# One order for the high and the low matmul of a weight tile, in every contraction step

## The chip, the cores and the metric

The kernel runs on one core of one Trainium2 chip. The metric is the device time of one execution in microseconds (us). A shorter stretch is given in nanoseconds (ns) where that reads better.

## What is computed

One transformer-like block on 256 tokens of 2048 features, depth 1, in fp32: a gated feed-forward layer, a hybrid mixer (a gated short convolution beside a chunked state-space scan), a second feed-forward layer, a per-layer embedding gate and a last norm.

```python
def swiglu(x, w_in, w_out):
    g, u = jnp.split(x @ w_in, 2, axis=-1)
    return (jax.nn.silu(g) * u) @ w_out

def reference(x, p, ...):
    h = x
    for i in range(DEPTH):
        h = h + 0.5 * swiglu(rmsnorm(h, ffn1_norm[i]), ffn1_w_in[i], ffn1_w_out[i])
        h = h + hybrid_mixer(rmsnorm(h, mix_norm[i]), mix_w_in[i], ...)
        h = h + 0.5 * swiglu(rmsnorm(h, ffn2_norm[i]), ffn2_w_in[i], ffn2_w_out[i])
        gate = jax.nn.sigmoid(rmsnorm(h, ple_norm[i]) @ ple_w_gate[i])
        h = h + gate * (p[i] @ ple_w_proj[i])
    return rmsnorm(h, final_norm)
```

The weights are large (the feed-forward width is 5632) and every weight is used once.

## The kernel before

Activations lie with features on the partitions and the 256 tokens along the free axis. To keep fp32 accuracy with the faster float32r products, each operand is split into a high part and a low part. An activation tile of the right-hand side holds both, 256 columns of high next to 256 columns of low. A weight chunk of four contraction tiles (128 x 4 x 256) is loaded by SyncE (L95), copied to its high part on ScalarE (`hi`, L99), and the low part is the difference, made on VectorE (`lo`, L100). There are four raw buffers and three buffers of each part.

`Gemm` (L104 to L133) accumulates 256 output features, two halves of 128 called j = 0 and 1, each in a PSUM bank of its own. For each contraction tile k of a chunk it issues two matmuls: `hi` times both halves of x, 512 columns, over the whole bank; and `lo` times the high half of x, 256 columns, into the bank's second half. The tile numbers of a Gemm run chunk by chunk, in a chunk first all k of j = 0 and then all k of j = 1. At the last contraction tile of an accumulation the two matmuls are swapped, so that the wide one comes last and carries the stop mark:

```python
todo = [(acc, wh, x), (acc[:, T:], wl, x[:, 0:T])]
if k == self.K - 1:
    todo.reverse()
```

In TensorE's queue that gives hi, lo, hi, lo and so on, and once in each accumulation lo, lo, hi, hi: the last two tiles' low matmuls next to each other, then the last high one next to the first high one of what follows. There are 391 such accumulations. Those of the feed-forward and the mixer's input projection have 14, 15 or 16 contraction tiles, those of the mixer's output projection 32. The tail of the program (`one=True`) and the small projection `pr` use three narrow matmuls of 256 columns and have no swap.

`gather` (L138) drains an accumulator: ScalarE reads its second half (`elo`, L141), VectorE adds the first (`esum`, L143). Accumulators are double-buffered. A norm has `nps` (TensorE, L185), `nv` (VectorE, L202), `nrt` (GpSimd, L204), `npb` (TensorE, L208) and `r` (L211) in a row, with a few products of the next Gemm placed between `nps` and `npb`. The scan of the mixer puts small fp32 matmuls (`cb`, `xt`, `st`, `ab`, `yp`) between stretches of the projection's products; `st` reads `xe` (VectorE, L350).

The program is written with a scheduling framework. It lays out each engine's queue before the run, from priorities and from its own estimate of when operands will be ready; the weight splits have a raised priority (L98). So an edit in one place can move instructions of other engines.

Of the kernel before, what the change touches and what calls it, by code (L numbers as in the profile page):

```python
# [14 lines left out]
P = 128  # L15
T = 256
# [9 lines left out]
KC = 4  # L26
NEG = -1.0e30

# column tiles of mix_w_in in the order in which they are computed
C_B, C_C, C_X, C_Z, C_XS, C_BM, C_CM, C_DT = 0, 2048, 4096, 6144, 8192, 10240, 10752, 11264  # L30
MIX_ORDER = [("bc", i, C_BM + i * P) for i in range(8)]
MIX_ORDER += [("xs", i, C_XS + i * P) for i in range(16)]
# [5 lines left out]
Z_ORDER = [("z", i, C_Z + i * P) for i in range(16)]  # L38
ALL_ORDER = MIX_ORDER + SC_ORDER + Z_ORDER

# columns of the packed per-feature parameters
S_N1, S_NM, S_N2, S_NP, S_NF, S_SN, S_D = (16 * i for i in range(7))
S_SC = 112
S_CW = S_SC + 48
# [5 lines left out]
def block_kernel(ctx, tc, xT, pT, small, dtp, w1, o1, wm, wdt, om, w2, o2, wg, wp, out):  # L50
# [12 lines left out]
    def aux(name):  # L63
        return aux_p.tile([P, 512], F32, tag="aux", name=name)

    # ---- inputs and constants
    warm = cst.tile([P, 1], F32, name="warm")
    V.memset(warm, 0.0)
    A.activation(out=warm, in_=warm, func=AF.Exp)
# [19 lines left out]
    half = cst.tile([P, 2], F32, name="half")  # L89
    G.memset(half, -0.5)  # L90

    # ---- weights: load, split into two float32r parts
    def parts(src, nk, cols):
        w = raw.tile([P, KC, 256], F32, tag="w", name="w")
        nc.sync.dma_start(out=w[:, :nk, :cols], in_=src)  # L95
# [6 lines left out]
        return hi, lo  # L102

    class Gemm:  # L104
        """src [P, K, cols]; rhs(k) -> [P, 512] (high | low). One bank per 128 columns:
        [:256] the high products, [256:] the cross products (or all of them in [:256])."""

        def __init__(self, src, K, rhs, cols=256, one=False, acc=None):
            self.src, self.K, self.rhs, self.cols, self.one = src, K, rhs, cols, one
# [2 lines left out]
        def chunk(self, k0, k1):  # L112
            hi, lo = parts(self.src[:, k0:k1, :], k1 - k0, self.cols)
            for j in range(self.cols // P):
                js = slice(j * P, (j + 1) * P)
                for k in range(k0, k1):
                    x, acc = self.rhs(k), self.acc[:, j, :]
                    wh, wl = hi[:, k - k0, js], lo[:, k - k0, js]
                    if self.one:
                        todo = [(acc[:, 0:T], wh, x[:, 0:T]), (acc[:, 0:T], wh, x[:, T:]),  # L120
                                (acc[:, 0:T], wl, x[:, 0:T])]
                    else:
                        todo = [(acc, wh, x), (acc[:, T:], wl, x[:, 0:T])]
                        if k == self.K - 1:
                            todo.reverse()
                    for n, (o, a, b) in enumerate(todo):
                        nc.tensor.matmul(o, lhsT=a, rhs=b, start=(k == 0 and n == 0),  # L127
                                         stop=(k == self.K - 1 and n == len(todo) - 1))
# [7 lines left out]
        return Gemm(*args, **kw).all()  # L136

    def gather(acc, n=2, scale=1.0):  # L138
        """The sum of an accumulator's two halves, times scale, in SBUF."""
        lo = ev.tile([P, 2, T], F32, tag="elo", name="elo")  # L140
        A.mul(out=lo[:, :n, :], in_=acc[:, :n, T:], mul=scale)  # L141
        s = ev.tile([P, 2, T], F32, tag="esum", name="esum")
        V.scalar_tensor_tensor(out=s[:, :n, :], in0=acc[:, :n, 0:T], scalar=scale,  # L143
                               in1=lo[:, :n, :], op0=ALU.mult, op1=ALU.add)
        return s

    def split(dst, src, w=None):
        """dst [P, 512] f32r = high | low part of src (times the column w)."""
        if w is None:
            A.copy(out=dst[:, 0:T], in_=src)  # L150
            V.tensor_tensor(out=dst[:, T:], in0=src, in1=dst[:, 0:T].bitcast(F32), op=ALU.subtract)
        else:
            A.activation(out=dst[:, 0:T], in_=src, func=AF.Copy, scale=w)
            V.scalar_tensor_tensor(out=dst[:, T:], in0=src, scalar=w,  # L154
                                   in1=dst[:, 0:T].bitcast(F32), op0=ALU.mult, op1=ALU.subtract)
# [7 lines left out]
        return r.unsqueeze(1).to_broadcast([P, 2, T])  # L163

    class Norm:
        """Sums squares over features as they come; r = 1/sqrt(mean + eps) over partitions."""

        def __init__(self, n, tag):
            self.n, self.tag, self.acc, self.more = n, tag, None, None
# [15 lines left out]
                nc.tensor.matmul(ps[c], lhsT=src[:, c * P:(c + 1) * P], rhs=ones[:, 0:1], start=start, stop=stop)  # L185

        def begin(self):
            """All but the last tile's share, ahead of it."""
            self.ps = [aux("nps")[:, 0:1] for _ in range(NCH)]
            self.total(self.acc, self.ps, True, False)  # L190

# [20 lines left out]
            return (pbs[0], r) if both else r  # L212

    def next_x(src, m, x, wcol, norm):
        """Two finished tiles of h: their squares, and their parts for the next product."""
        norm.add(src)
        if x is not None:
            for i in range(2):
                split(x(m + i), src[:, i, :], sm[:, wcol + m + i:wcol + m + i + 1])

    # ---- feed-forward
    def ffn(wi, wo, x, norm, wcol_next, begun=()):
        xn, nn, r = None, Norm(D, "rn"), None
        f0 = 0
# [35 lines left out]
    for m in range(0, KD, 2):  # L260
        n1.add(h[:, m:m + 2, :])
    xm, nm = ffn(w1, o1, x1, n1, S_NM, first)
    # ---- mixer
    XT = blk.tile([P, KD, T], F32, tag="blk", name="XT")
    Xd = blk.tile([P, NCH, D], F32, tag="blk", name="Xd")
    ya = [blk.tile([P, 8, 512], F32R, tag="blk", name=f"ya{i}") for i in range(2)]
    BC = tmp.tile([P, 8, T], F32, name="BC")

    def conv(dst, src, wcol, taps, bias=None, func=None):
        """Causal over the free axis, one feature a partition."""  # L270
        c = ev.tile([P, T], F32, tag="t1", bufs=5, name="cv")
        w = lambda i: sm[:, wcol + i:wcol + i + 1]
        t = dst if func is None else c
        if bias is None:
            A.activation(out=t, in_=src, func=AF.Copy, scale=w(taps - 1))
        else:
            A.activation(out=t, in_=src, func=AF.Identity, scale=w(taps - 1), bias=bias)
        for d in range(1, taps):
            V.scalar_tensor_tensor(out=t[:, d:], in0=src[:, :T - d], scalar=w(taps - 1 - d),
                                   in1=t[:, d:], op0=ALU.mult, op1=ALU.add)  # L280
        if func is not None:
            A.activation(out=dst, in_=t, func=func)
# [17 lines left out]
            dst = XT[:, q, :] if kind == "xs" else BC[:, q, :]  # L300
            conv(dst, s[:, j, :], S_CW + 4 * ch, 4, bias=sm[:, S_CB + ch:S_CB + ch + 1], func=AF.Silu)

    # step sizes, in [head, token]
    s = gather(gemm(wdt, KD, xm, cols=P), n=1)
    dx = ev.tile([HEADS, T], F32, tag="t1", bufs=5, name="dx")
    V.tensor_tensor(out=dx, in0=s[:HEADS, 0, :], in1=rm[:HEADS, :], op=ALU.mult)
# [4 lines left out]
    an = tmp.tile([HEADS, 1], F32, name="an")  # L311
    A.activation(out=an, in_=dtv[:, 1:2], func=AF.Exp)
    V.tensor_scalar(out=an, in0=an, scalar1=-1.0, scalar2=None, op0=ALU.mult)
    # log(1 + e) = 2 atanh(e / (2 + e))
    sr = ev.tile([HEADS, T], F32, tag="t1", bufs=5, name="sr")
    V.tensor_scalar(out=sr, in0=e, scalar1=2.0, scalar2=None, op0=ALU.add)
    V.reciprocal(out=sr, in_=sr)
# [11 lines left out]
    V.tensor_scalar(out=dA, in0=dt, scalar1=an, scalar2=None, op0=ALU.mult)  # L329

    def ssd_group(g):
        # B C^T of the group, [s, l], and its B with tokens on partitions
        ps = aux("cb")
        for c in range(NCH):
            cs = slice(c * P, (c + 1) * P)
            nc.tensor.matmul(ps[:, cs], lhsT=BC[:, g, cs], rhs=BC[:, 4 + g, cs], start=True, stop=True)  # L336
        nc.tensor.transpose(ps[:, T:T + P], BC[:, g, 0:P], ident)
        CB = tmp.tile([P, 3, P], F32, tag="CB", bufs=2, name="CB")
        A.copy(out=CB.rearrange("p c l -> p (c l)"), in_=ps[:, 0:3 * P])
        for c in range(NCH):  # L340
            ps = aux("xt")
            for j in range(4):
                nc.tensor.transpose(ps[:, j * P:(j + 1) * P], XT[:, 4 * g + j, c * P:(c + 1) * P], ident)  # L343
            V.tensor_tensor(
                out=Xd[:, c, g * 512:(g + 1) * 512].rearrange("p (h d) -> p h d", d=HD),
                in0=ps.rearrange("p (h d) -> p h d", d=HD),
                in1=dtT[:, c, 0, g * 8:(g + 1) * 8].unsqueeze(2).to_broadcast([P, 8, HD]),
                op=ALU.mult)
        xe = ev.tile([P, 512], F32, tag="xe", bufs=1, name="xe")
        V.tensor_tensor(  # L350
            out=xe.rearrange("p (h d) -> p h d", d=HD),
            in0=Xd[:, 0, g * 512:(g + 1) * 512].rearrange("p (h d) -> p h d", d=HD),
            in1=dec[:, g * 8:(g + 1) * 8].unsqueeze(2).to_broadcast([P, 8, HD]),
            op=ALU.mult)
        ps = aux("st")
        nc.tensor.matmul(ps, lhsT=CB[:, 2, :], rhs=xe, start=True, stop=True)  # L356
        st = ev.tile([P, 512], F32, tag="st", bufs=1, name="st")
        A.copy(out=st, in_=ps)
        return CB, st
# [36 lines left out]
                in1=yp[:, a].rearrange("p c l -> p (c l)"), op0=ALU.mult, op1=ALU.add)  # L396

    def token_major():
        # token-major steps, and their running sums
        ps = aux("dtT")  # L400
        for c in range(NCH):
            for i, t in enumerate((dt, dA, dA)):
# [5 lines left out]
        for c in range(NCH):  # L408
            nc.tensor.matmul(ps[:, c * HEADS:(c + 1) * HEADS], lhsT=tri, rhs=dtT[:, c, 1, :], start=True, stop=True)
        for c in range(NCH):  # L410
            # running sums by head, twice over the partitions
            nc.tensor.matmul(ps[0:2 * HEADS, T + c * P:T + (c + 1) * P],
                             lhsT=dtT[:, c, 1:3, :].rearrange("p i h -> p (i h)"), rhs=tri,
                             start=True, stop=True)
# [8 lines left out]
        A.activation(out=dec, in_=ps[:, 2 * HEADS:3 * HEADS], func=AF.Exp)  # L423
        return dtT, acs, dec, sums

    # gated short convolution, the scan beside it
    for j in range(0, 16, 2):
        cvs = ev.tile([P, 2, T], F32, tag="cvs", bufs=1, name="cvs")
        for i in range(2):
# [16 lines left out]
            gst = ssd_group(g)  # L446
        ssd_heads(g, hh, *gst)

    # gate and group norm
    yb = []  # L450

    def group_norm(g, ng):
# [31 lines left out]
        V.tensor_tensor(out=hm, in0=s, in1=hm, op=ALU.add)  # L484
        next_x(hm, m, x2, S_N2, n2)

    # ---- second feed-forward
    xp, np_ = ffn(w2, o2, x2, n2, S_NP)

    # ---- per-layer embedding gate, final norm  # L490
    nf, rp = Norm(D, "rn"), None
    pin = ev.tile([P, 2, T], F32, tag="xe", bufs=1, name="pin")
    G.dma_start(out=pin, in_=pT)
# [47 lines left out]


def _layout(inp):
    """The inputs in the order in which the chip reads them: slices, transposes, repeats."""
    import numpy as np

    c = np.ascontiguousarray

    def tiled(w):
        """[K, N] -> [N/256, 128, K/128, 256]"""  # L550
        k, n = w.shape
        return c(w.reshape(k // P, P, n // 256, 256).transpose(2, 1, 0, 3))

    def gated(w):
        """Columns of gate and value side by side, 128 of each."""
        k = w.shape[0]
        return c(w.reshape(k // P, P, 2, KF, P).transpose(3, 1, 0, 2, 4)).reshape(KF, P, k // P, 256)

    def feat(v, per=1):
        """[per, F] -> [128, F/128 * per]"""  # L560
        v = np.asarray(v).reshape(per, -1, P)
        return v.transpose(2, 1, 0).reshape(P, -1)

# [39 lines left out]
```

## Time and profile before

| what | value |
|---|---|
| median of three timed runs | 2353.78 us (2353.03 to 2354.49) |
| the profiled execution, first to last instruction (span) | 2350.7 us |
| that execution's own device time | not listed; the median lies 3.1 us above the span |
| TensorE busy with matmuls | 2328.5 us, 99% of the span, 13,340 matmuls |
| TensorE loading weights | 2014.7 us, 86% |
| VectorE, ScalarE, GpSimd busy | 64%, 48%, 1% |
| granted TensorE clock, mean | 0.998 of full speed |
| mean busy share of the DMA queue that loads the weights (q1) | 60.6% |

The page's busy time of TensorE counts a matmul from its start to a modelled end, so matmuls overlap; what a matmul costs is read from the distance of its start to the next one's start.

### The profile page before, as it was taken

The numbers are of one execution on the slowest core, as the hardware profiler recorded it, in microseconds if no ns is written. First come the engines' busy times: TensorE is split into PE (matmuls) and PEld (weight loads), VectorE is DVE, ScalarE is ACT, GpSimd is POOL, SyncE is SP. The second block draws the span as 40 slices with busy tenths as digits, with TensorE's granted clock in tenths as the row PEclk, the third lists the DMA queues.
The fourth block names the chain that finished last, engine by engine and source line by source line (L and its number), as shares of the span: only waits on it lengthen the run. The fifth ranks groups of instructions, "written<-read, shape, count | busy, mean of one in ns | idle before, by whom it ended". The sixth has DMA issues, their size and how long they took to land.

```text
span 2350.7 us, 33760 instructions
## 1 busy us (share of the span) xinstructions
PE 2328.5 (99%) x13340; PEld 2014.7 (86%) x13340; DVE 1500.9 (64%) x1928; ACT 1135.4 (48%) x1491; POOL 12.8 (1%) x25
## 2 busy tenths in 40 slices
PE   8999999999999999999999999999999999999998
PEld 7888888888888888888888888888888888888887
DVE  7665566655667777777767655566556655666766
ACT  6444444444445555444445444444444444444553
POOL 0000000000000000000000000000000000000000
PEclk9999999999999999999999999999999999999999
DMA  7666666666666565555555566666666666666654
GB/s 236 187 186 183 190 186 187 184 190 185 186 179 192 181 188 179 158 160 170 166 173 177 175 186 186 182 186 187 186 187 186 187 187 184 189 187 179 189 180 139
DMA packets 126864, 429.39 MB, mean 183 GB/s; under 512 B 13617, under 2 KB 20017, under 8 KB 126705
## 3 DMA queue, kind: packets, MB, share of 16 engines
q1 hardware_dynamic: 126144, 426.17, 60.6%
q8 instruction: 104, 1.70, 0.3%
q10 hardware_dynamic: 480, 0.80, 0.1%
q14 instruction: 56, 0.45, 0.1%
q0 software_dynamic: 80, 0.26, 0.0%
HBM read 425.08 MB, written 2.10 MB: 182 GB/s over the span
## 4 chain that ended last, share of the span: by engine, by line
PE 99%; POOL 0%; issue 0%; DMA 0%; DVE 0%; ACT 0%; POOLq 0%; DVEq 0%
PE acc L127 96%; PE pr L127 0%; PE yp L388 0%; POOL nrt L204 0%; PE yp L391 0%; PE npb L208 0%; PE ab L367 0%; DMA sm<-in_small 0%; PE st L356 0%; PE xt L343 0%; PE nps L185 0%; POOL hw L531 0%; PE cb L336 0%; DVE nv L202 0%; DVE xa L154 0%
## 5 line engine op out<-in xcount | busy, mean ns | idle before, releaser
L100 DVE TENSOR_TENSOR lo<-w,hi 128x1024 fp32r<-128x1024 f32 (+1 forms) x834 | 990.8, 1189 | 724.8 <-ACT hi L99 715.4
L99 ACT CAST hi<-w 128x1024 fp32r<-128x1024 f32 (+1 forms) x834 | 850.4, 1020 | 966.4 <-PE acc L127 752.7
L127 PE MATMUL acc<-xa,hi 128*128 128x512 f32 (+1 forms) x2264 | 802.9, 398 | 6.4 <-DVE xa L154 6.4
L127 PE MATMUL acc<-xb,hi 128*128 128x512 f32 (+1 forms) x2264 | 796.6, 397 | 0.0
L127 PE MATMUL acc<-xa,lo 128*128 128x256 f32 x2248 | 633.6, 282 | 0.0
L127 PE MATMUL acc<-xb,lo 128*128 128x256 f32 x2248 | 588.8, 282 | 0.0
L127 PEld LDWEIGHTS acc<-xa,hi 128*128 128x128 f32 x2264 | 425.0, 188 | 102.8 <-ACT hi L99 6.4
L127 PEld LDWEIGHTS acc<-xb,hi 128*128 128x128 f32 x2264 | 415.2, 188 | 81.8 <-issue 0.3
L127 PEld LDWEIGHTS acc<-xb,lo 128*128 128x128 f32 x2248 | 424.5, 189 | 23.8 <-issue 3.1
L127 PEld LDWEIGHTS acc<-xa,lo 128*128 128x128 f32 x2248 | 425.8, 189 | 7.9 <-DVE lo L100 0.9
L127 PE MATMUL acc<-ga,hi 128*128 128x512 f32 x768 | 273.3, 398 | 0.0
L127 PE MATMUL acc<-gb,hi 128*128 128x512 f32 x640 | 226.7, 398 | 0.0
L127 PE MATMUL acc<-ga,lo 128*128 128x256 f32 x768 | 215.7, 281 | 0.0
L127 PEld LDWEIGHTS acc<-ga,hi 128*128 128x128 f32 x768 | 144.3, 188 | 33.5
L127 PE MATMUL acc<-gb,lo 128*128 128x256 f32 x640 | 164.0, 281 | 0.0
L143 DVE SCALAR_TENSOR_TENSOR esum<-acc,elo 128x512 f32<-128x512 f32 (+1 forms) x196 | 133.9, 683 | 25.5 <-ACT elo L141 25.2
L141 ACT ACTIVATE elo<-acc 128x512 f32<-128x512 f32 (+1 forms) x196 | 115.9, 591 | 67.2 <-PE acc L127 67.2
L127 PEld LDWEIGHTS acc<-ga,lo 128*128 128x128 f32 x768 | 145.2, 189 | 2.2
L127 PEld LDWEIGHTS acc<-gb,hi 128*128 128x128 f32 x640 | 117.1, 188 | 23.2
L127 PEld LDWEIGHTS acc<-gb,lo 128*128 128x128 f32 x640 | 120.7, 189 | 6.6
L127 PE MATMUL acc<-ya,hi 128*128 128x512 f32 x256 | 90.7, 398 | 0.0
L127 PE MATMUL acc<-yb,hi 128*128 128x512 f32 x256 | 90.3, 398 | 0.0
(142 smaller groups left out, 1134.2 us busy)
## 6 DMA issues: line engine op xcount, KB each, us to landing
w<-in_w SPq DMA_DIRECT2D x350, 512.0 KB, 4.4
w<-in_wm SPq DMA_DIRECT2D x176, 512.0 KB, 3.8
w<-in_o SPq DMA_DIRECT2D x144, 512.0 KB, 3.6
w<-in_om SPq DMA_DIRECT2D x64, 512.0 KB, 4.0
w<-in_wg SPq DMA_DIRECT2D x28, 512.0 KB, 4.6
w<-in_o SPq DMA_DIRECT2D x32, 384.0 KB, 3.5
w<-in_o SPq DMA_DIRECT2D x16, 256.0 KB, 3.0
w<-in_wp SPq DMA_DIRECT2D x8, 256.0 KB, 2.7
```

The source lines that it names most:

```text
L99: A.copy(out=hi[:, :nk, :cols], in_=w[:, :nk, :cols])
L100: V.tensor_tensor(out=lo[:, :nk, :cols], in0=w[:, :nk, :cols], in1=hi[:, :nk, :cols].bitcast(F32), op=ALU.subtract)
L127: nc.tensor.matmul(o, lhsT=a, rhs=b, start=(k == 0 and n == 0), stop=(k == self.K - 1 and n == len(todo) - 1))
L141: A.mul(out=lo[:, :n, :], in_=acc[:, :n, T:], mul=scale)
L143: V.scalar_tensor_tensor(out=s[:, :n, :], in0=acc[:, :n, 0:T], scalar=scale, in1=lo[:, :n, :], op0=ALU.mult, op1=ALU.add)
```

## The change

The swap at the last contraction tile goes. Every contraction tile has its high matmul first and its low one second, and the stop mark of an accumulation sits on a matmul of 256 columns. Comments and doc strings were removed too, and below L125 the line numbers are two lower.

```diff
                     else:
                         todo = [(acc, wh, x), (acc[:, T:], wl, x[:, 0:T])]
-                        if k == self.K - 1:
-                            todo.reverse()
                     for n, (o, a, b) in enumerate(todo):
                         nc.tensor.matmul(o, lhsT=a, rhs=b, start=(k == 0 and n == 0),
                                          stop=(k == self.K - 1 and n == len(todo) - 1))
```

The number of instructions on each engine is the same. What moves, at the places that matter:

TensorE, the end of an accumulation in the first feed-forward layer, before (`gb` is the gated activation, `x2` two such rows in a run):

```order
L127 MATMUL acc<-gb,hi 128x512
L127 MATMUL acc<-gb,lo 128x256 x2
L127 MATMUL acc<-gb,hi 128x512 x2
L127 MATMUL acc<-gb,lo 128x256
L127 MATMUL acc<-gb,hi 128x512
```

and with the change:

```order
L125 MATMUL acc<-gb,hi 128x512
L125 MATMUL acc<-gb,lo 128x256
L125 MATMUL acc<-gb,hi 128x512
L125 MATMUL acc<-gb,lo 128x256
L125 MATMUL acc<-gb,hi 128x512
L125 MATMUL acc<-gb,lo 128x256
L125 MATMUL acc<-gb,hi 128x512
```

The doubled rows are gone: high and low matmuls alternate through the end of the accumulation, and through all other ends too, until a matmul of another kind comes.

VectorE at the norm of a group of the mixer (its first one), before:

```order
L202 TENSOR_SCALAR nv<-nps 128x2
L143 SCALAR_TENSOR_TENSOR esum<-acc,elo 128x512
L211 COPY r<-npb 128x256
L100 TENSOR_TENSOR lo<-w,hi 128x1024
L458 SCALAR_TENSOR_TENSOR yn<-XT,sm,r 128x256 x4
```

and with the change:

```order
L200 TENSOR_SCALAR nv<-nps 128x2
L100 TENSOR_TENSOR lo<-w,hi 128x1024
L141 SCALAR_TENSOR_TENSOR esum<-acc,elo 128x512
L209 COPY r<-npb 128x256
L470 TENSOR_TENSOR esum<-esum,r 128x512
```

The weight split `lo` now stands right behind `nv`, ahead of `esum`. The same move is made at the norm that opens the mixer and at the two group norms that follow, four places in all; at the last group norm `lo` followed `nv` before already.

ScalarE in the scan, ahead of the state copy `st` of the second group, before:

```order
L275 ACTIVATE cvs<-v,sm 128x256
L99 CAST hi<-w 128x1024 x2
L141 ACTIVATE elo<-acc 128x512
L99 CAST hi<-w 128x1024 x2
L150 CAST ya_6757<-cvs 128x256 x2
L358 COPY st<-st 128x512
```

and with the change:

```order
L273 ACTIVATE cvs<-v,sm 128x256
L99 CAST hi<-w 128x1024 x3
L139 ACTIVATE elo<-acc 128x512
L356 COPY st<-st 128x512
L99 CAST hi<-w 128x1024
L148 CAST ya_6757<-cvs 128x256 x2
```

The drain `elo` stands behind one more weight copy. That holds nearly all through the mixer and the second feed-forward layer, and from the last third of the first one on; before that ScalarE's order is the same. On VectorE `xe` moved up by one place there (`Xd`, `Xd`, `esum`, `xe` in place of `Xd`, `esum`, `Xd`, `cvs`, `xe`), and on TensorE `st` stands 14 products behind the `xt` transposes where it stood 17. On TensorE the small matmuls of the scan's first group and those of the last group norm also stand 8 to 16 products from where they stood. The queues of SyncE and GpSimd are unchanged.

## Rows read from the trace of the kernel before

**Rows 1.** The chain of work that ended last, by line, first row of that view

```profile
by line: PE acc L127 96.5%; PE pr L127 0.5%; PE yp L388 0.4%; POOL nrt L204 0.3%; PE yp L391 0.3%; PE npb L208 0.2%; PE ab L367 0.2%; issue 0.2%; DMA sm<-in_small 0.2%; PE st L356 0.1%; PE xt L343 0.1%; PE nps L185 0.1%; POOL hw L531 0.1%; 
```

**Rows 2.** The same chain's long pieces: start us, us, what (x matmuls)

```profile
32.96 734.19 PE acc L127 x4158
769.23 150.27 PE acc L127 x852
...
950.50 23.97 PE acc L127 x135
...
985.11 27.12 PE acc L127 x153
...
1026.12 24.85 PE acc L127 x141
...
1311.63 185.10 PE acc L127 x1051
1498.86 745.26 PE acc L127 x4221
```

**Rows 3.** Timeline of TensorE, mixer's output projection, fourth Gemm: start us, us

```profile
1372.98 0.40 PE L127 MATMUL acc<-ya,hi 128*128 128x512 f32 x1
...
1392.77 0.40 PE L127 MATMUL acc<-yb,hi 128*128 128x512 f32 x1
```

**Rows 4.** The same matmuls of the Gemm that begins at 1327.47 us

```profile
1328.17 0.39 PE L127 MATMUL acc<-ya,hi 128*128 128x512 f32 x1
...
1347.59 0.39 PE L127 MATMUL acc<-yb,hi 128*128 128x512 f32 x1
```

**Rows 5.** Timeline of TensorE behind the norm that opens the mixer

```profile
769.53 0.40 PE L127 MATMUL acc<-xa,hi 128*128 128x512 f32 x1
...
777.51 0.39 PE L127 MATMUL acc<-xb,hi 128*128 128x512 f32 x1
777.74 0.40 PE L127 MATMUL acc<-xb,lo 128*128 128x256 f32 x2
...
779.97 0.40 PE L127 MATMUL acc<-xa,hi 128*128 128x512 f32 x1
...
788.80 0.40 PE L127 MATMUL acc<-xb,hi 128*128 128x512 f32 x1
```

**Rows 6.** Timeline of TensorE behind the scan's last yp of a group

```profile
985.96 0.39 PE L127 MATMUL acc<-xb,hi 128*128 128x512 f32 x1
...
987.35 0.39 PE L127 MATMUL acc<-xb,hi 128*128 128x512 f32 x1
987.58 0.40 PE L127 MATMUL acc<-xb,lo 128*128 128x256 f32 x2
```

**Rows 7.** Timelines of ScalarE, VectorE, TensorE in the scan's second group

```profile
1012.26 0.60 ACT L141 ACTIVATE elo<-acc 128x512 f32<-128x512 f32 x1 [1.85 <-PE acc L127]
1012.76 1.04 ACT L99 CAST hi<-w 128x1024 fp32r<-128x1024 f32 x1
...
1013.91 0.68 DVE L344 TENSOR_TENSOR Xd<-xt,dtT 128x512 f32<-128x512 f32 x1
...
1015.10 0.69 DVE L350 TENSOR_TENSOR xe<-Xd,dec 128x512 f32<-128x512 f32 x1
...
1015.95 1.02 PE L356 MATMUL st<-xe,CB 128*128 128x512 f32 x2
```

**Rows 8.** Timelines of GpSimd and VectorE at two norms

```profile
1309.22 1.64 POOL L204 TENSOR_TENSOR nrt<-nv,half 128x2 f32<-128x2 f32 x1 [18.36 <-DVE nv L202]
...
1309.09 1.23 DVE L100 TENSOR_TENSOR lo<-w,hi 128x1024 fp32r<-128x1024 f32 x1
...
1497.41 0.69 POOL L204 TENSOR_TENSOR nrt<-nv,half 128x2 f32<-128x2 f32 x1 [186.55 <-DVE nv L202]
...
1497.84 1.23 DVE L100 TENSOR_TENSOR lo<-w,hi 128x1024 fp32r<-128x1024 f32 x1 [0.51 <-ACT hi L99]
```

## The prediction

> **What bounds the kernel now.** I read the chain of waits first. 96.5% of the chain is the one line that issues the Gemm products [rows 1], and its pieces are long and unbroken: 4158 matmuls without a wait in the first feed-forward layer, 4221 in the second [rows 2]. So the time is the number of products times the distance from one start to the next. The edit removes no product; it can act through that distance, or through a small piece of the chain that is not a product.
>
> Then I read the timeline of TensorE to see whether the distance is constant. It is not: the same instructions run in two rhythms. In the fourth Gemm of the mixer's output projection two high matmuls 56 pairs apart start 19.79 us apart, 353.4 ns a pair [rows 3]. The same two matmuls of the second Gemm lie 19.42 us apart, 346.8 ns a pair [rows 4]. The granted clock, the data rate and the neighbours are alike; I call them the slow and the fast rhythm. Seven of the eight Gemms of that stage show the slow one.
>
> A rhythm seems to be set where TensorE begins a stretch, and kept until the order is broken. Behind the norm that opens the mixer, 23 pairs take 7.98 us, 347.0 ns each; then comes the swap (two low matmuls in a row), and 25 pairs of the next Gemm take 8.83 us, 353.2 ns each [rows 5]. Behind the scan's small matmuls the rhythm is fast again, 4 pairs in 1.39 us (347.5 ns), until the swap at 987.58 us [rows 6]. I found no stretch in which it changed without a swap or a matmul of another kind, over 56 pairs and more. So the swap, which the change removes, is what ends a fast stretch, and nearly every stretch now ends up slow: 734.19 us / 4158 x 2 is 353.1 ns a pair, 745.26 / 4221 x 2 is 353.1 [rows 2].
>
> **The change part by part.** All is against the profiled execution, span 2350.7 us; the median of the timed runs lies 3.1 us above that, and I carry the differences over to it.
>
> *The swap itself.* If a slow stretch stays slow, its mean goes from the one with swaps in it, 353.1 ns a pair, to the unbroken one, 353.4 ns. That is +0.25 ns on 2079 pairs, +0.5 us, in the first feed-forward layer, and +0.6 us on 2110 pairs in the second. The output projection now has 352.2 ns (185.10 / 1051 x 2) and would have 353.4: 525 pairs, +0.6 us, of which the lost fast Gemm is over half [rows 2 to 4]. Together +1.7 us. The starts are rounded to 10 ns, so the difference of the two means is uncertain by about as much as it is: bounds 0 and +3 us.
>
> *Stretches that begin fast and now stay fast.* Priced at 346.8 ns a pair [rows 4] against what they take now [rows 2]:
> the mixer's first stretch, 426 pairs: 150.27 - 147.73 = 2.5 us;
> the four stretches of 153 matmuls, each 27.12 - 26.53 = 0.59, together 2.4 us;
> the three of 141, each 24.85 - 24.45 = 0.40, together 1.2 us;
> the one of 135: 23.97 - 23.41 = 0.6 us.
> Sum -6.7 us. The lower bound of this part is that none keeps its rhythm (0). The upper one is that every long stretch catches the fast one: 2079 pairs x 6.4 ns is 13.2 us in the first feed-forward layer, 13.4 in the second, 2.9 in the output projection, 36 us in all with the above. I take the entries as the profile shows them, since the instructions ahead of each stretch stay the same: the two feed-forward layers and the output projection begin slow, the mixer and the stretches behind `yp` fast. The small matmuls of the scan's first group move, so its part is the least sure.
>
> *The drains.* `elo` stands behind one more weight copy, so it starts about 1 us later (1.04 us for the copy, which followed it before [rows 7]); the accumulator is needed again a whole Gemm later, 16 pairs twice over or 11 us. Cost 0. If that cover were gone, TensorE would wait for the drain at the next but one Gemm. For `st`, three products sooner is 0.53 us (three at 177 ns); `xe` moves up past one VectorE operation (`cvs`), which gives back 0.6 us, from 1013.91 to 1015.10 for two places. `esum` stands ahead of it and needs `elo`. The copy would begin where `elo` began, at 1012.26 or a little sooner, and with 1.04 and 0.60 us the two end by 1013.9; the second `Xd`, moved up one place, ends at 1013.91 + 0.68 - 0.60 = 1014.0, and only then does VectorE come to `esum` [rows 7]. Cost 0, bounds -0.5 and +0.5 us for each of the four groups.
>
> *The norms.* `npb` waits for `nrt`, GpSimd's power. `nrt` took 0.69 us where `lo` began after it, at 1497.84 against 1497.41, and 1.64 us where `lo` had begun before it, at 1309.09 against 1309.22 [rows 8]. With the change `lo` follows `nv` at four more norms. There the weight copy it needs is released only by the end of the same Gemm, as at 1497, so `lo` should start some 0.3 to 0.4 us after `nrt`, and nothing is lost. Cost 0, bounds -1.0 (at the last group norm, where 0.13 us decide) and +3.8 us (four times 0.95).
>
> Sum: +1.7 - 6.7 = -5.0 us, so 2353.8 - 5.0 = **2348.8 us**. A measurement of this kernel can tell about 0.2%, 4.7 us, from no change. The forecast lies just past that line, and the lesser uncertainties decide on which side it falls.
>
> **The rivals.**
>
> *A feed-forward layer catches the fast rhythm.* Both layers begin behind a norm, where TensorE waits for GpSimd and starts at an arbitrary moment. Of the stretches behind such a norm one began fast [rows 5] and the others slow, so a start is fast perhaps one time in six or seven. With the change that decides over 13.7 us (13.2 and the 0.5 not added): 2335.1 us, and 2321 with both. For it: nothing in the new order would break a rhythm for 734 us. Against: both layers began slow in this profile.
>
> *The rhythm does not hold, or order does not matter.* Something other than the swap, such as the waits for a new weight chunk, might bring back the slow rhythm within a Gemm's length; my longest unbroken fast piece is one Gemm. Then all is slow: 2353.8 + 1.7 = 2355.5 us, a little slower than before. The Trainium skill speaks for such a result: "TensorE: Matmul & The Clock Gate", section "Back-to-back issue gap", gives a matmul of N columns at full clock N / 2.4 + 2.5 ns behind any other, an estimate of 325 ns a pair in any order, so that the change would be worth 0. The trace agrees with neither figure nor constancy: 346.8 and 353.4 ns for the same pair [rows 3, 4].
>
> *The split holds up the power.* If at the four norms `lo` starts before `nrt`, each `npb` comes 0.95 us later: 2348.8 + 3.8 = 2352.6 us. It decides by whether the weight copy ends before `nv`. The Trainium skill, "SBUF — State Buffer", section "Who interferes with whom", states the rule: VectorE with two operands from SBUF and a GpSimd operation that reads SBUF exclude each other, and whichever issues first runs to its end. The two norms agree [rows 8].
>
> *The drain sticks behind a copy that waits* (slower). In the scan the copy that now stands ahead of `elo` might wait not for the Gemm's end but for the next chunk's end, eight pairs or 2.83 us later. Then `esum`, `xe` and `st` come that much later, in each of four groups: 2348.8 + 11.3 = 2360.1 us. It decides from the point at which `elo` ends after the second `Xd`. Against it: before, that copy ran right behind `elo` without a wait of its own [rows 7], so it was free at the Gemm's end.
>
> That the order isn't what the source says can be excluded: the queue shows the alternation.
>
> **How the numbers follow.** The forecast has 0.40, a fast feed-forward layer 0.20, no lasting rhythm 0.27, the split ahead of the power 0.06, the stuck drain 0.07. The time is that of the forecast. The range 2333 to 2357 us takes in a single fast feed-forward layer (2335.1) and the slow rhythm throughout (2355.5) with the bounds of the swap's own cost; it leaves out two fast layers and most of the stuck drain, about 0.12 in all. Given the forecast, a little over half lies beyond 4.7 us, 0.21; with 0.20 for a fast layer that is faster 0.42 in round numbers. No lasting rhythm, the split and the rest of the forecast fall within the line, 0.50. Slower is the stuck drain and the upper edge of the slow rhythm, 0.08.
>
> **What would show it.** Right: in the timeline, the mixer's first stretch (about 850 products) takes 147.7 us, 346.8 ns a pair to its end; the stretches of 153 and 141 take 26.5 and 24.5 us; the two feed-forward layers stay at 353.4 ns. Wrong: a stretch that begins fast and turns slow with no other matmul between; a feed-forward layer at 346.8 ns; an `nrt` of 1.64 us at 768, 1242, 1266 or 1290 us; `st` idle for `xe`. The step most likely to fail is the one on entries, that a stretch begins in the rhythm in which it began before.

## The result, and the profile after

In the first comparison the changed kernel took 2337.33 us (median of 6 executions, 2335.19 to 2349.98) and the kernel before 2353.41 us (6 executions, 2351.55 to 2354.49); the ratio is 0.9947, 95% interval 0.9934 to 0.9959. A second comparison gave 2348.82 us (12 executions, 2334.47 to 2352.66) against 2353.62, ratio 0.9968, interval 0.9952 to 0.9984. So the change makes the kernel faster by some 0.3 to 0.5%. The changed kernel's executions don't scatter about one value, though: of these 18, eight lie between 2334.5 and 2338.8 us, ten between 2348.4 and 2352.7, none between. A median over a few of them says mostly which cluster they fell into.

The first profiled execution of the changed kernel belongs to the lower cluster (2338.82 us, span 2337.1). Its chain of waits, long pieces of the Gemm line (start us, us, what, x matmuls), beside [rows 2]:

```profile
33.34 734.59 PE acc L125 x4158
...
770.00 123.67 PE acc L125 x700
...
900.42 18.07 PE acc L125 x103
...
986.61 26.67 PE acc L125 x153
...
1027.28 25.04 PE acc L125 x141
1062.98 27.17 PE acc L125 x153
...
1315.45 180.93 PE acc L125 x1035
1498.53 731.60 PE acc L125 x4221
```

The second feed-forward layer has the same 4221 products as before and takes 731.60 us for 745.26: 346.6 ns a pair, the fast rhythm, to its end. The first has 734.59 for 734.19, the slow rhythm without the swaps. The books of the span, 2350.7 to 2337.1, by the starts of these pieces here and in [rows 2] (the norm between the first layer and the mixer, 2.1 us in both, is not listed):

| stretch | before, us | after, us | difference |
|---|---|---|---|
| start to the first layer | 32.96 | 33.34 | +0.4 |
| first feed-forward layer | 734.19 | 734.59 | +0.4 |
| mixer, from its first piece to the second layer | 729.63 | 728.53 | -1.1 |
| second feed-forward layer | 745.26 | 731.60 | -13.7 |
| from its end to the end | 106.6 | 107.0 | +0.4 |

Nearly all of it is one layer. The mixer gains in the output projection, which begins with a few products at a lower clock and is fast behind them (180.93 / 1035 x 2 is 349.6 ns a pair with those in it). It gives a part of that back in its first stretch: the head, fast for 23 pairs before [rows 5], is now slow (123.67 / 700 x 2 is 353.3 ns; an estimate of 0.15 us, 23 pairs at 6.5 ns), and TensorE waits there for a weight part (below). Two smaller things stand beside that.

GpSimd at the norms (start us, us, operation, idle time ahead of it and its releaser), beside [rows 8]:

```profile
768.54 0.69 POOL L202 TENSOR_TENSOR nrt<-nv,half 128x2 f32<-128x2 f32 x1 [735.97 <-DVE nv L200]
...
1243.47 0.71 POOL L202 TENSOR_TENSOR nrt<-nv,half 128x2 f32<-128x2 f32 x1 [71.29 <-DVE nv L200]
1267.67 0.69 POOL L202 TENSOR_TENSOR nrt<-nv,half 128x2 f32<-128x2 f32 x1 [23.48 <-DVE nv L200]
1291.43 0.69 POOL L202 TENSOR_TENSOR nrt<-nv,half 128x2 f32<-128x2 f32 x1 [23.08 <-DVE nv L200]
1313.04 1.64 POOL L202 TENSOR_TENSOR nrt<-nv,half 128x2 f32<-128x2 f32 x1 [20.92 <-DVE nv L200]
```

At the four norms where `lo` moved up, the power still takes 0.7 us. On VectorE `lo` starts there behind it, not ahead (start us, us, operation):

```profile
768.30 0.16 DVE L200 TENSOR_SCALAR nv<-nps 128x2 f32<-128x2 f32 x1 [0.93 <-PE nps L183]
768.92 1.23 DVE L100 TENSOR_TENSOR lo<-w,hi 128x1024 fp32r<-128x1024 f32 x1 [0.46 <-ACT hi L99]
```

The idle time ahead of `lo` ends with the weight copy, and `lo` starts 0.38 us behind the power, too late to hinder it (0.35 to 0.36 us at the other three). At the last group norm nothing changed.

And one wait has grown. TensorE's timeline near the end of the mixer's first stretch, and VectorE's and ScalarE's (same columns):

```profile
899.27 0.39 PE L125 MATMUL acc<-xa,hi 128*128 128x512 f32 x1
900.42 0.38 PE L125 MATMUL acc<-xa,lo 128*128 128x256 f32 x1 [0.76 <-DVE lo L100]
...
896.40 1.10 ACT L275 ACTIVATE cv<-esum,sm 128x256 f32<-128x256 f32 x2 [0.67 <-DVE esum L294]
897.40 1.98 ACT L99 CAST hi<-w 128x1024 fp32r<-128x1024 f32 x2
...
897.04 2.19 DVE L277 SCALAR_TENSOR_TENSOR cv<-esum,sm,cv 128x255 f32<-128x255 f32 x5
899.14 1.22 DVE L100 TENSOR_TENSOR lo<-w,hi 128x1024 fp32r<-128x1024 f32 x1
```

Here, around the Gemm of half width, the convolution's `cv` stands ahead of the weight copies on ScalarE and of the split on VectorE, and TensorE waits 0.76 us for `lo`. At the same place in the kernel before, a weight load (PEld) waited too, but briefly:

```profile
901.16 0.40 PE L127 MATMUL acc<-xa,hi 128*128 128x512 f32 x1
901.44 0.19 PEld L127 LDWEIGHTS acc<-xa,lo 128*128 128x128 f32 x1 [0.21 <-DVE lo L100]
901.45 0.38 PE L127 MATMUL acc<-xa,lo 128*128 128x256 f32 x1
```

The low matmul starts 0.29 us behind its high one, where 0.23 to 0.24 is usual, and the next high one is late as well, together some 0.15 us. In both traces TensorE is in the slow rhythm ahead of this wait and in the fast one behind it, with no swap and no other matmul between.

### The profile page after: what moved, and what is told of

Read it like the earlier page. It is cut to its first block, busy times and chain, and to the rows that moved or that the text cites. A ratio compares the mean times of both kernels' runs of the same rounds, so it can differ in the third digit from the quotient of the medians.

```text
span 2337.1 us, 33615 instructions
## 1 busy us (share of the span) xinstructions
PE 2314.5 (99%) x13340; PEld 2014.2 (86%) x13340; DVE 1509.3 (65%) x1928; ACT 1134.8 (49%) x1491; POOL 12.8 (1%) x25
## 4 chain that ended last, share of the span: by engine, by line
PE 98%; POOL 0%; DVE 0%; issue 0%; DMA 0%; ACT 0%; POOLq 0%; DVEq 0%
PE acc L125 96%; PE pr L125 0%; PE yp L386 0%; POOL nrt L202 0%; PE yp L389 0%; PE npb L206 0%; PE ab L365 0%; DMA sm<-in_small 0%; PE xt L341 0%; PE nps L183 0%; PE st L354 0%; POOL hw L529 0%; DVE cv L277 0%; DVE lo L100 0%; PE cb L334 0%
## 5 line engine op out<-in xcount | busy, mean ns | idle before, releaser
L125 PE MATMUL acc<-xa,hi 128*128 128x512 f32 (+1 forms) x2264 | 800.1, 396 | 5.9 <-DVE xa L152 5.9
L125 PE MATMUL acc<-xb,hi 128*128 128x512 f32 (+1 forms) x2264 | 795.7, 394 | 0.0
L125 PE MATMUL acc<-xa,lo 128*128 128x256 f32 x2248 | 632.3, 281 | 0.8 <-DVE lo L100 0.8
L125 PE MATMUL acc<-xb,lo 128*128 128x256 f32 x2248 | 632.7, 281 | 0.0
L125 PEld LDWEIGHTS acc<-xa,hi 128*128 128x128 f32 x2264 | 424.9, 188 | 105.8 <-ACT hi L99 5.9
L125 PEld LDWEIGHTS acc<-xb,hi 128*128 128x128 f32 x2264 | 423.6, 188 | 98.2
L125 PEld LDWEIGHTS acc<-xa,lo 128*128 128x128 f32 x2248 | 426.0, 189 | 1.7 <-DVE lo L100 1.5
L125 PEld LDWEIGHTS acc<-xb,lo 128*128 128x128 f32 x2248 | 424.7, 189 | 3.1 <-issue 2.9
L125 PE MATMUL acc<-ga,hi 128*128 128x512 f32 x768 | 270.9, 395 | 0.0
L125 PE MATMUL acc<-gb,hi 128*128 128x512 f32 x640 | 226.3, 395 | 0.0
L125 PE MATMUL acc<-ga,lo 128*128 128x256 f32 x768 | 215.4, 280 | 0.0
L125 PE MATMUL acc<-gb,lo 128*128 128x256 f32 x640 | 179.5, 280 | 0.0
L125 PEld LDWEIGHTS acc<-ga,hi 128*128 128x128 f32 x768 | 144.0, 187 | 33.8
L125 PEld LDWEIGHTS acc<-ga,lo 128*128 128x128 f32 x768 | 145.1, 189 | 0.0
L125 PEld LDWEIGHTS acc<-gb,hi 128*128 128x128 f32 x640 | 120.0, 187 | 28.1
L125 PEld LDWEIGHTS acc<-gb,lo 128*128 128x128 f32 x640 | 120.9, 189 | 0.0
L125 PE MATMUL acc<-ya,hi 128*128 128x512 f32 x256 | 90.5, 395 | 0.0
L125 PE MATMUL acc<-yb,hi 128*128 128x512 f32 x256 | 89.4, 392 | 0.0
```

## The experiments

The theory that the trace of before suggested, sharpened by the trace after: **theory 1**, TensorE runs the pair in one of two rhythms; a start behind other work draws one, and it lasts while high and low alternate; what a swap leads to depends on where in the rhythm it falls, and so on its distance from the last one. **Theory 2**: the gain comes from what else changed at an accumulation's end (the narrow last matmul, drains and splits in another order). **Theory 3**: rhythms come by chance, and a swap ends but does not choose one. Each edit is to the changed kernel.

The distances that theory 1 rests on, in nanoseconds from start to start, read from the trace's starts of the matmuls (H: behind a high one, l: behind a low one; a bar marks a swap, that is l then l, H then H):

```
fast, unbroken        H230 l117 H230 l116 H230 l117                       346.7 a pair
slow, unbroken        H236 l113 H233 l117 H241 l120                       353.3 a pair, every three pairs the same
before, swap 4 apart  l120 | l120 H236 | H233 l114 H232 l118 H241 l120 | l120 H235 | H234 l113 H233 l117 H241 l120
3 pairs apart         l120 | l120 H236 | H233 l114 H232 l118 | l121 H237 | H235 l117 H235 l116 H230 l117 H230 l117
before, behind l113   H236 l113 | l119 H234 | H235 l116 H224 l118 H233 l118 | l121 H237 | H235 l116 H235 l117 H230 l117 H230 l117
```

The slow rhythm repeats every three pairs. A swap that falls behind its l120 starts the same cycle anew. One that falls a pair earlier, behind l118, leads into the fast rhythm. The last row is the end of the output projection's first Gemm in the kernel before: its first swap falls behind an l113, so the second, again four pairs later, falls behind an l118, and the Gemm of [rows 4] is fast. So the place in the cycle decides; the distance does so only where the last swap set the cycle.

**The swap in the middle of an accumulation.**

```diff
                         todo = [(acc, wh, x), (acc[:, T:], wl, x[:, 0:T])]
+                        if k == 8:
+                            todo.reverse()
```

> Edit to the changed kernel: at the ninth contraction tile (k = 8) of every accumulation low and high are exchanged, so the swap is back, as often as before, but in the middle of an accumulation; its end stays as the change left it (low matmul last, narrow matmul with the stop mark, drains and splits in the changed order; ScalarE's, VectorE's and GpSimd's queues are the same). Theory 1 (the rhythm is set by entries and swaps, and kept while high and low alternate): nearly every stretch is slow again, 353 ns a pair; 2350 to 2355 us, and the two clusters of the changed kernel (2335 to 2339 and 2349.5 to 2350) are gone. Theory 2 (the gain comes from the accumulation's end: the narrow last matmul, the earlier drains, the moved splits): as the changed kernel, 2335 to 2350 us in two clusters.

Measured: 2353.08 us (11 executions, 2351.47 to 2353.46) against 2354.20 of before, ratio 0.9997 (0.9989 to 1.0006). Chain of its profile, the two feed-forward layers:

```profile
33.06 732.87 PE acc L127 x4158
...
1499.47 743.96 PE acc L127 x4221
```

The swap alone brings the time of before back, with the accumulation's end left as changed. By the trace's starts both layers began fast (the second at 346.7 ns a pair) and were slow from their first swaps on. Theory 2 falls, and so do drains, splits and stop mark as the source of the gain.

**Four swaps at the head of four long stretches, and three.** One Gemm near the head of each layer, of the mixer's first stretch and of the output projection gets `kick=KICK`:

```diff
+KICK = (9, 13, 17, 20)
...
+                        if self.pair in self.kick:
+                            todo.reverse()
+                        self.pair += 1
```

> Edit to the changed kernel: no swaps but four in a row at the head of each of four long stretches (both feed-forward layers, the mixer's first stretch, the output projection), at pairs 9, 13, 17 and 20 of one Gemm; 16 pairs of 13,340 matmuls are exchanged and nothing else moves. Theory 1 in its strict form (two rhythms, and a swap carries from one to the other by the place in the rhythm where it falls: a swap four pairs behind another leads into slow, one three pairs behind another into fast): whatever the entry, all four stretches run at 346.8 ns a pair behind the fourth swap, 734.7 - 13.5 = 721 us in the first feed-forward layer, 731.7 in the second, 147.9 in the mixer's first stretch; 2320 to 2324 us, all executions within 4 us of each other. Theory 2 (end of the accumulation): as the changed kernel, 2335 to 2350 in two clusters. Theory 3 (a stretch's rhythm is drawn at random, swaps end it but do not choose): feed-forward layers fast or slow by chance, spread over 14 to 28 us.

The other kernel has `KICK = (9, 13, 17)`.

> As the kernel with four swaps at the head of four long stretches, but without the fourth: swaps at pairs 9, 13 and 17 alone, four pairs apart. Theory 1 in its strict form: all four stretches are slow to their ends, 734.7 us in the first feed-forward layer and 745.3 in the second, 353.4 ns a pair; 2353 to 2356 us in one cluster. Theory 2: as the changed kernel, 2335 to 2350 in two clusters. Theory 3: spread by chance over 14 to 28 us, like the one with four swaps. The two kernels differ by four exchanged pairs, and theory 1 puts some 32 us between them.

Measured with four: 2321.90 us (4 executions, 2321.76 to 2322.44), ratio 0.9865 (0.9851 to 0.9878). With three: 2355.58 us (11 executions, 2353.79 to 2356.44), ratio 1.0006 (0.9997 to 1.0015). The chain with four, long pieces:

```profile
34.08 720.84 PE acc L130 x4158
...
756.99 121.44 PE acc L130 x700
...
1300.51 179.44 PE acc L130 x1035
1482.09 731.68 PE acc L130 x4221
```

and with three:

```profile
33.38 734.56 PE acc L130 x4158
...
770.01 123.64 PE acc L130 x700
...
1316.94 182.49 PE acc L130 x1035
1501.58 745.61 PE acc L130 x4221
```

Four exchanged pairs are worth 33.7 us: every one of the four stretches is fast with the fourth swap and slow without it. Theory 3 falls with the spread it asked for. By the starts, the second layer and the output projection of the kernel with three began fast, and its swaps turned them slow. Its first layer is also the test of what three swaps cost by themselves: slow with them at 734.56 us, slow without them at 734.59, so nothing that can be told.

**A swap at every second contraction tile.**

```diff
+                        if k % 2 == 1:
+                            todo.reverse()
```

> Edit to the changed kernel: every second contraction tile has its low matmul first, so that TensorE's queue reads high, low, low, high, high, low, low, high throughout, and a swap falls on every pair. Theory 1 in its strict form, with the distances that the traces show behind a swap (235 to 237 ns behind a wide matmul, 116 to 121 behind a narrow one): one rhythm only, 348.3 ns a pair whatever the entry, about 2328 us (2322 to 2336), all executions within 4 us. Theory 2: as the changed kernel or, with the swap back at the ends, as the one before: 2335 to 2354.

Measured: 2327.82 us (4 executions, 2327.18 to 2330.14), ratio 0.9893 (0.9878 to 0.9908). Its first layer:

```profile
32.76 724.24 PE acc L127 x4158
```

724.24 / 4158 x 2 is 348.4 ns a pair, expected 348.3. Swaps on every pair, and still 26 us faster than before: a swap is not dear, its place decides. Where the number of contraction tiles is even, the accumulations end here as in the kernel before, with the wide matmul, and still are not slow: theory 2 falls a second time.

**As many swaps as before, three pairs apart in place of four.**

```diff
+            last = {0: (self.K - 1, self.K - 2), 3: (self.K - 1, self.K - 1), 2: (self.K - 2, self.K - 1)}[self.K % KC]
...
+                        if k == last[j]:
+                            todo.reverse()
```

> As many swaps as the kernel before has, one in each accumulation, but the one of the second half stands three pairs behind that of the first half instead of four (at the last contraction tile of the first half and the last but one of the second, where there are 16). Theory 1 in its strict form (a swap four pairs behind another leads into slow, three behind into fast, and any swap in a fast stretch into slow): every Gemm is slow for three pairs and fast for the other 27 to 29; with some 27 ns for the pairs around the swaps of each of 195 Gemms 2325 us (2322 to 2330), in one cluster. The prediction's wording (a swap ends a fast stretch, and what follows is slow): 2353 to 2356, as before.

Measured: 2325.00 us (4 executions, 2323.42 to 2326.56), ratio 0.9882 (0.9869 to 0.9894). Its first layer:

```profile
32.80 723.01 PE acc L128 x4158
```

So what made the kernel before slow is that its two swaps of a Gemm with 16 contraction tiles stand 4 and then 28 pairs apart, and both are one more than a multiple of three: each falls behind l120 again. (Where there are 15 tiles they stand 3 and 27 apart; there, by the trace's starts, the first leads out of the slow rhythm and the second, three pairs later, back into it. Where there are 14 they stand 2 and 26 apart; there the first falls behind an l113, and the layer stays slow.)

**One swap more in a fast layer.**

```diff
-                acc = begun[f].acc if f0 + f < len(begun) else gemm(wi[f0 + f], KD, x, kick=KICK if f0 + f == (2 if begun else 1) else ())
+                acc = begun[f].acc if f0 + f < len(begun) else gemm(wi[f0 + f], KD, x, kick=KICK if f0 + f == (2 if begun else 1) else (20,) if f0 + f == 22 and not begun else ())
```

> The kernel with four swaps at the heads of four long stretches, and one single swap more, in the middle of the second feed-forward layer (its 23rd Gemm, pair 20, some 1146 of 2110 pairs before the end). Theory 1: the layer runs at 346.7 ns a pair up to that swap and at 353.4 to its end behind it, 731.7 + 1146 x 6.64 = 739.3 us for the layer, 2329.5 us in all against 2321.9. A theory by which a swap costs only itself: 2321.9 as without it.

Measured: 2329.44 us (4 executions, 2329.09 to 2330.03). The layer's piece of the chain, and TensorE's timeline at the swap:

```profile
1480.95 739.54 PE acc L130 x4221
```

```profile
1802.72 0.39 PE L130 MATMUL acc<-xb,hi 128*128 128x512 f32 x1
1802.95 0.28 PE L130 MATMUL acc<-xb,lo 128*128 128x256 f32 x1
1803.06 0.39 PE L130 MATMUL acc<-xb,hi 128*128 128x512 f32 x1
1803.29 0.40 PE L130 MATMUL acc<-xb,lo 128*128 128x256 f32 x2
1803.53 0.62 PE L130 MATMUL acc<-xb,hi 128*128 128x512 f32 x2
```

From the trace's starts the layer runs at 346.6 ns a pair up to this swap and at 353.2 behind it. One exchanged pair costs 7.5 us (2329.44 against 2321.90), about as expected.

**The changed kernel again.**

> The changed kernel again, unedited, to see how often a feed-forward layer catches the fast rhythm. Theory 1 (drawn anew at each execution where TensorE re-enters behind a norm): the executions fall into clusters 13.5 to 14 us apart, near 2321 (both layers fast), 2335 to 2339 (one) and 2349 to 2350 (none), and both the middle and the upper one occur; in the six executions so far it was four to two. Theory 2 (the first run's executions were of two kinds for another reason, such as the half clock behind the last group norm): a continuous spread, or clusters at other distances.

Measured as told above: 4 of 12 executions in the lower cluster, and none near 2321 us, where both layers would be fast. Two pieces of the chain of its profiled execution (2334.47 us):

```profile
33.17 734.58 PE acc L125 x4158
...
1494.19 731.60 PE acc L125 x4221
```

Two more single executions:

> The changed kernel once more, for a profile of an execution of the upper cluster (10 of 18 so far). Theory 1: if its time is 2348 to 2353, the second feed-forward layer is one stretch of 4221 products in 745.6 us, 353.3 ns a pair, against 731.6 in the two profiles of the middle cluster; if it is 2334 to 2339, 731.6 again. If the clusters come from another place, the layer takes 731.6 us in either case.

> The same kernel and the same two cases as the run before it: 2348 to 2353 with the second feed-forward layer at 745.6 us, or 2334 to 2339 with 731.6. The first layer decides over 13.7 us as well: 720.9 us in place of 734.6 would show it fast, which no profile of the changed kernel has shown.

Measured: 2352.47 and 2343.85 us. The second is a value between the clusters, which was not expected. The chain of the first, three pieces:

```profile
33.45 734.58 PE acc L125 x4158
770.11 121.36 PE acc L125 x700
...
1498.73 745.65 PE acc L125 x4221
```

and of the second:

```profile
34.26 734.58 PE acc L125 x4158
770.91 123.67 PE acc L125 x700
...
1317.40 183.94 PE acc L125 x1035
1503.48 731.60 PE acc L125 x4221
```

In the profiled executions the clusters are the second layer's rhythm: 745.65 us where the execution took 2352.47, 731.60 where it took 2343.85, as in the other two profiles. For the 16 executions without a profile that is inferred from their times. The mixer's first stretch is drawn too, 121.36 us in one and 123.67 in the other. The execution of 2343.85 us has a fast second layer, and lost 5.0 us of span against the first profile elsewhere: 0.9 ahead of the first layer, 1.0 between the mixer's start and the output projection, 3.0 in the projection, which drew the slow rhythm. It also began at a lower clock, as the first profile's did. Rows by time there (us, length, busy time and count of PE, PEld, DVE, ACT, POOL, then the granted TensorE clock, the DMA share and GB/s):

```profile
1316.00:1318.00 2.00, 1.72 (x7) 1.63 (x8) 0.53 (x2) 0.00 (x0) 0.22 (x1) 0.61 0.66 166
1318.00:1320.00 2.00, 2.00 (x9) 1.71 (x8) 1.90 (x5) 0.41 (x1) 0.00 (x0) 0.54 0.33 129
```

**The four swaps at the head of 15 stretches.**

```diff
+HEADS_OF = (65, 2147, 2643, 2724, 2827, 2916, 3019, 3108, 3211, 3300, 3379, 3443, 3507, 3563, 4083)
+KICK = {s + i for s in HEADS_OF for i in (2, 6, 10, 13)}
...
+                        if pairs[0] in KICK:
+                            todo.reverse()
+                        pairs[0] += 1
```

> The changed kernel with the four swaps (the fourth three pairs behind the third) at the head of each of 15 stretches between other matmuls, those of the scan, the gate and the group norms too; 60 pairs are exchanged and nothing else moves. Theory 1: of the nine short stretches that were slow in the kernel with four such heads each gives back some 0.4 us (50 to 63 pairs at 6.6 ns), together 3.5 us, less some 0.1 us in each that was fast already: 2318.5 us (2317 to 2320.5), against 2321.9. If short stretches have no rhythm to keep: 2321.9 or a little above.

Measured: 2319.51 us (4 executions, 2318.44 to 2320.22), ratio 0.9858 (0.9845 to 0.9871), the fastest version here. Its chain, the stretch of 141 products that took 25.04 us in the changed kernel:

```profile
1011.43 24.69 PE acc L132 x141
```

The expected time was 2318.5. The nine short stretches that were slow gave back 0.26 to 0.42 us each, 3.1 us in all where 3.5 was expected, and the two of 153 that were fast already pay 0.1 us each, as expected (26.75 for 26.67). Where the rest of the 1.0 us lies was not traced.

## Why the prediction was right, and where it failed

**The mechanism held.** Two rhythms for the same instructions, kept while the order alternates, and the swap as what ends a fast stretch: the exchange in the middle, the single swap in a fast layer and the pair of kernels with four and three swaps show each of these alone. The range held both medians, but the forecast of 2348.8 us is met by the second alone; the first lies 11.5 us below it. The direction was right as well, though 0.50 stood on no change that can be told and 0.42 on faster.

**What it had too wide** is the swap as such. By its wording (a swap ends a fast stretch, and what follows is slow) the kernel with as many swaps, three pairs apart, would have taken 2353 to 2356 us; it took 2325.00, and the one with a swap on every pair 2327.82. A swap leads into either rhythm, by where it falls. Nor is a swap or another matmul needed: the prediction says that it found no stretch that changed without one, and its own trace has one, at the weight load that waits at 901.44 us.

**The swap itself**, +1.7 us: the slow first layer takes 734.58 to 734.59 us for 734.19, +0.4 where +0.5 was worked out, and the slow second 745.65 for 745.26, +0.4 for +0.6. The kernel with three swaps, in which both layers, the mixer's first stretch and the output projection are slow, is 1.4 us above before; its interval takes in no change.

**The step that failed is the one on entries**, which the prediction named as the likeliest to fail: that a stretch begins in the rhythm in which it began before. The instructions ahead of a stretch are the same, but the draw is not fixed by them. The second layer, forecast slow, was fast in three of four profiles. The mixer's first stretch, forecast to give 2.5 us, was fast in two of four, and there it took 2.3 us less than in the slow ones. The stretches of 141 were forecast at 24.5 us and took 25.04 in all four profiles, more than the 24.85 of before; two of the four stretches of 153 stayed slow at 27.17 in the first profile. In the kernel before, these stretches begin one and a half pairs ahead of a swap, so no rhythm of the entry could be read there, and what made them 24.85 is a fast Gemm behind their second swap (347.1 ns a pair by the trace's starts). So the -6.7 us of the forecast came only in part, and the -13.7 us of the rival came in its place.

**A feed-forward layer catches the fast rhythm** was that rival, at 2335.1 us and a chance of 0.20 from one start in six. Its price was right (731.60 for 745.26, and a lower cluster of 2334.5 to 2338.8). Its chance was too small for the second layer, eight of 18 timed executions if those without a profile are like those with one, and too large for the first, which took 734.58 to 734.59 us in all four profiles. The two layers do not seem to share one chance. The upper cluster, 2348.4 to 2352.7, is the forecast with part of its terms; that its value of 2348.8 is also the second comparison's median is luck, by how the draws fell.

**The rhythm does not hold, or order does not matter** was too high at 0.27: it held for 731 us. Two orders of the same matmuls in the kernels with four and three swaps lie 33.7 us apart. What the rival got right is that a wait for a weight can change the rhythm: in the mixer's first stretch it did so in the kernel before and in the first profile of the changed one, both times from slow to fast. The Trainium skill's "TensorE: Matmul & The Clock Gate", section "Back-to-back issue gap", has a formula in which the distance depends on the columns and the clock alone, and calls it that of an isolated matmul. The estimate of 325 ns a pair that the prediction took from it does not agree with the 346.7, 348.4 and 353.4 ns measured at a mean granted clock of 0.997 to 0.998, and one figure cannot stand for all these orders.

**The split holds up the power** did not happen, for the reason that the prediction gave: `lo` waits for the weight copy, and starts 0.35 to 0.38 us behind `nrt`. The traces show one side only of the exclusion that the prediction names: the power is longer behind a split, but `lo` takes 1.23 us whether a power has just begun or not. **The drain behind a waiting copy** did not happen either. In the scan's second group `elo` now starts later, but `esum` and `xe` follow without a gap; VectorE and TensorE there, beside [rows 7]:

```profile
1013.76 1.29 DVE L342 TENSOR_TENSOR Xd<-xt,dtT 128x512 f32<-128x512 f32 x2 [0.98 <-PE xt L341]
1014.96 0.68 DVE L141 SCALAR_TENSOR_TENSOR esum<-acc,elo 128x512 f32<-128x512 f32 x1
1015.56 0.68 DVE L348 TENSOR_TENSOR xe<-Xd,dec 128x512 f32<-128x512 f32 x1
...
1016.46 1.02 PE L354 MATMUL st<-xe,CB 128*128 128x512 f32 x2
```

`st` starts 0.90 us behind the start of `xe` (0.85 before) and TensorE doesn't wait for it.

**Not foreseen**: the 0.76 us for `lo` at the Gemm of half width, for which the 0.21 us of the weight load at 901.44 in the kernel before was the sign. The moved drains were priced by when their own buffer is needed; what they and `cv` push back on ScalarE, the next weight copies, was looked at in the scan alone.

## What to carry to other kernels

Where one engine issues without a wait for hundreds of microseconds, read the distance from start to start at several places before pricing an edit: a mean can hide two levels, and then an edit is worth what it does to the level, not what it adds. The period of the slower level says which order keeps it (here swaps 4 and 28 pairs apart) and which leaves it (here one three pairs behind another), and a few exchanged instructions at the head of a stretch can choose what is otherwise left to chance: with the swaps of before gone, 60 exchanged pairs of some 6,400 made this kernel 1.4% faster than before. Judge a kernel with such clusters by its clusters, with a dozen executions, not by the median of a few.

## What was not expected of the hardware

- The two rhythms themselves, 346.7 and 353.3 ns for a high and a low matmul at full granted clock, each lasting over 700 us once begun, and the rule by which a swap leads from one to the other. Why the slow one has a period of three pairs, and what in a start draws the rhythm, was not tried and stays open. In the first layer the draw was slow in every profile of the kernel before and of the changed one, but in the kernel with the swap in the middle of the accumulation that layer began fast. A wait of TensorE for a weight part can draw anew: in the four profiles of the changed kernel it led from slow into fast once, from slow into slow once, and left the fast rhythm fast twice.
- The output projection begins behind a wait of TensorE of about 1.75 us from product to `npb`, in the kernel before as in the changed one. In two of the four profiles of the changed kernel, and in the kernel with swaps three pairs apart, the granted clock then stood at 0.50 of full speed, which is the level of 1.2 GHz, for some 3 us, with high matmuls 0.64 us apart. In the other two and in the kernel before, with the same wait, it stayed at 1.00. Its price is 1.2 us in the slow rhythm (183.94 us against 182.79 for the same 1035 products) and 1.6 in the fast one (180.93 against 179.36). What decides it is open.
